# A two-level Strassen MLP kernel: a new written-out order of a pair, some sums moved to GpSimd, other buffers, and more of the second matmul begun in the drain

## The chip, the cores and the metric

The kernel runs on one core of a Trainium2 chip. TensorE (PE in the profile) does the matrix products, VectorE (DVE) and ScalarE (ACT) the work on their results, GpSimd (POOL) some element-wise sums and the stores, and SyncE (SP) issues the loads. The metric is the device time of one execution in microseconds (us), the median of the runs shown. Before the change it is 1467.58 us over three runs, from 1467.18 to 1467.59 us.

## The reference

Eight batches of 1024 rows go through a two-layer perceptron; everything is float32 outside and float16 inside the products.

```python
x: (8, 1024, 1024)   w1: (1024, 4096)   w2: (4096, 1024)
h = x @ w1
h = 0.5 * h * (1 + np.tanh(np.sqrt(2 / np.pi) * (h + 0.044715 * h ** 3)))
return (h @ w2).astype(np.float32)
```

## The kernel before

**Stages.** The eight batches are eight steps. Steps 0 and 1 use a one-level Strassen-Winograd scheme (seven block products in place of eight) and, beside it, prepare the sums of weights in DRAM. Steps 2 to 7 use two levels: each of the seven block products is again made of seven smaller ones. These six late steps are the same code: `matmul1_late` (L766) for x @ w1 with the GELU, then `matmul2` (L1113).

**The first matmul of a late step** goes over eight *pairs* j = 0..7 (a pair is 2 x 128 columns of each half of w1). The order of every instruction in a pair is written out by hand in the list `PAIR` (L30). One pass over the list is one pair; a token with a prime (') belongs to the pair before, so that the end of one pair lies among the beginning of the next. After pair 7 the list is gone through once more for its primed tokens alone: the *drain*. The instructions of each engine keep the order of the list. The tokens that matter here:

- `m` and two digits: one small product on TensorE, two matmuls of 256 columns (L704); `h`: four matmuls of 512 columns (L489). In pair 0 the products 1, 5 and 7 are not split; they are four matmuls of 512 columns per half (`whole`, L669).
- `z`, `e`, `s`, `u`: sums on VectorE that take a result out of a PSUM bank or put it into another; a following `m` that writes this bank again must wait for them. `c`, `a`, `p`, `q`: copies on ScalarE. `g`: the GELU on ScalarE into the tiles g11, g12, g21, g22.
- `v`: a sum on GpSimd; `d`: the difference of two chunks of g11 and g21, on GpSimd except in the first and the last pair (L758).
- `k`: a sum of weights, made on GpSimd for the next pair (L298). `b`: one quarter of the sum s7 of the second matmul, on GpSimd, in pairs 4 to 7 (L782, L1037).
- `x` and two digits: one inner sum of x on VectorE (`inner_sum`, L337). It is made once in a step: in pair 0 without a prime, in pair 1 with one. The inner sums of x2 are made ahead; in step 2 those of x3 too. The rest, 16 in steps 3 to 7, lie in pairs 0 and 1.

**The second matmul** has seven products in the order 4, 1, 2, 5, 6, 7, 3, and each has seven steps of 16 matmuls of 256 columns (`Inner.steps`, L1068). The sums it needs (`a`) and other VectorE jobs are placed behind given steps by the table `FILL_2` (L62). `n6` and `n3` there make x6 and x3 of the next batch; they stand behind the steps (3,6) and (3,7), the last two of all. Product 4 is begun early: four quarters of its first step are put into the drain in front of the tokens in `BEGIN` (L37). Its third step needs the sum s6, which VectorE makes as one instruction (`a46`) after the drain, behind the last pair's `d`.

**Buffers.** `up` has 26 buffers of 4 KB per partition (loads, operands, sums of weights), `gc` 5 of 4 KB (inner sums of x, s sums, staging of float32 weights in step 0), PSUM 8 banks. A load into `up` is issued as soon as a buffer is free.

Of the kernel before, what the change touches and what calls it, by code (L numbers as in the profile page):

```python
# [9 lines left out]
DT = mybir.dt.float16  # L10
# [50 lines left out]

FILL_2 = slots("""00:a46 a45  # L62
    ;41:a43;42:a17;43:a16;44:a15;45:a13;46:i2
# [4 lines left out]
    ;71:y11 y12;72:y21 y22;73:a37;74:a36 w11;75:a35 w12;76:a33 w21;77:w22  # L68
    ;31:z11 z12;32:z21 z22;36:n6;37:n3""".replace("\n    ", ""))


@with_exitstack
def kernel(
# [192 lines left out]
    class StoredHalf:  # L266
# [20 lines left out]
        def two(self, ks):  # L287
            two = self.room.pop(0) if self.room else up.tile([P, 2, KH * 2 * P], DT, name="u")
# [27 lines left out]
    class XOps(dict):  # L316
# [19 lines left out]

        def inner_sum(self, m, j):  # L337
            if m not in self.inner:
                self.inner[m] = gcp.tile([P, 4, 2, HT // 2], DT, name="gc")

            def operand(b):
                if isinstance(b, int):
                    return self.inner[m][:, SUMS.index(b)]
                k, t = int(b[0]) - 1, int(b[1]) - 1
                return self[m][:, 2 * k:2 * k + 2, t * HT // 2:(t + 1) * HT // 2]

            u, op, v = W_SUM[j]
            tt(operand(j), operand(u), operand(v), op, True)

# [314 lines left out]
    class Pair:  # L664
# [48 lines left out]
        def run(self, key):  # L713
# [34 lines left out]
            elif kind in "apq":  # L748
                act_copy(temp(kind, m), bank("a" if kind == "a" else "c", m))
            elif kind == "s":  # L750
                tt(temp("s", m), bank("a", m), temp("p", m), SUB, True)
            elif kind == "u":
                add(temp("p", m), bank("f", m), temp("s", m))
            elif kind == "v":
                t = temp("q", m)
                tc.keep_in_program_order(nc.gpsimd.tensor_tensor(out=t, in0=t, in1=temp("p", m), op=ADD))  # L756
            elif kind == "d":
                spare = 0 < self.j < NI // 2 - 1  # L758
                difference(self.g, self.j, nc.gpsimd if spare else nc.vector)
            else:  # L760
                b, h = key[1:3], int(key[3])
                src = {"11": bank, "12": bank, "21": temp, "22": temp}[b]
                src = src({"11": "b", "12": "d", "21": "q", "22": "p"}[b], h)
                gelu_into(self.g[b][:, 2 * self.j + h, :], src, -1.0 if b == "12" else 1.0)

    def matmul1_late(xs, sb, quads, g):  # L766
# [5 lines left out]
        for j in range(n + 1):  # L772
# [3 lines left out]
            for key in PAIR:  # L776
                late = key.count("'")
                key = key.rstrip("'")
                if key[0] == "x":
                    if late == j and int(key[1]) not in made:  # L780
                        xs.inner_sum(int(key[1]), int(key[2]))
                elif key == "b":  # L782
                    if 4 <= j < n:
                        early.quarter(j - 4)
                elif key[0] == "k":
# [220 lines left out]
    class Inner:  # L1006


        def __init__(self, m, t, rows=lambda a, t: None, part=lambda b, t: None, base=None):
            self.m, self.rows, self.part, self.base = m, rows, part, base  # L1010
            self.begun = None
            self.x, self.s, self.y = {b: inner_block(t, b) for b in BLOCKS}, {}, {}
# [17 lines left out]

        def make(self, j):
            u, op, v = S_SUM[j]
# [4 lines left out]
        def quarter(self, i):  # L1037

            if i == 0:
                self.s[7] = gcp.tile([P, NI // 2, HT // 2], GT, name="gc")  # L1040
            u, op, v = S_SUM[7]
            out, in0, in1 = (t[:, 2 * i:2 * i + 2, :] for t in (self.s[7], self.x[u], self.x[v]))
            tc.keep_in_program_order(nc.gpsimd.tensor_tensor(out=out, in0=in0, in1=in1, op=op))

        def multiply(self, j, bank, first):
            for n in range(4):
# [21 lines left out]
        def steps(self, into):  # L1068

            a, b, c = self.begun or psum(), psum(), psum()  # L1070
            for n, (j, bank, first, out, adds) in enumerate((
# [7 lines left out]
            ), 1):  # L1079
                if n > 1 or self.begun is None:  # L1080
                    self.multiply(j, bank, first)
                if out is not None:
                    t = quarter(into, out)
# [26 lines left out]
    def half():  # L1110
        return up.tile([P, 2, OH], F32, name="u")

    def matmul2(sb, g, early, nxt):  # L1113
# [21 lines left out]
        def run(key):  # L1135
            for job in FILL_2.get(key, ()):
# [3 lines left out]
                elif kind == "g":  # L1140
# [5 lines left out]
                    else:  # L1146
                        tt(g12, g12, g22, SUB, True)
                elif kind == "w":
                    add(4, 1, b)
# [12 lines left out]

        def claim():

            t = half()
            act_copy(t[:, 0, :1], warm)
            return t

        order = (4, 1, 2, 5, 6, 7, 3)
# [3 lines left out]
        for m, after in zip(order, order[1:] + (None,)):  # L1173
            into[m] = into[1] if m == 6 else [claim(), claim()]
            if after is not None:
# [62 lines left out]
```

## Time and profile before

| what | value |
|---|---|
| median of three runs | 1467.58 us |
| the profiled execution | 1467.73 us, of which the span of its instructions is 1466.0 us |
| busy share: PE / DVE / ACT / POOL | 99% / 84% / 46% / 39% |
| granted TensorE clock | 0.999 |
| one late step, from one first matmul to the next | 176.5 us |
| DMA | 472.70 MB, 322 GB/s |

Busy time is the time in which at least one instruction of an engine is in flight. Matmuls are pipelined, so that a PE that is busy all the time may still start its matmuls too late; the loss is read from the distance of their starts. In a run without a wait this distance is 0.216 us for 512 columns and 0.109 us for 256. In the timeline, a row gathers neighbouring instructions of one kind; the number in brackets is the idle time ahead of it and what ended it.

### The profile page before, as it was taken

The numbers are of one execution on the slowest core, as the hardware profiler recorded it, in microseconds if no ns is written. First come the engines' busy times: TensorE is split into PE (matmuls) and PEld (weight loads), VectorE is DVE, ScalarE is ACT, GpSimd is POOL, SyncE is SP. The second block draws the span as 40 slices with busy tenths as digits, with TensorE's granted clock in tenths as the row PEclk, the third lists the DMA queues.
The fourth block names the chain that finished last, engine by engine and source line by source line (L and its number), as shares of the span: only waits on it lengthen the run. The fifth ranks groups of instructions, "written<-read, shape, count | busy, mean of one in ns | idle before, by whom it ended". The sixth has DMA issues, their size and how long they took to land.

```text
span 1466.0 us, 28773 instructions
## 1 busy us (share of the span) xinstructions
PE 1455.0 (99%) x10635; PEld 1038.6 (71%) x10635; DVE 1227.9 (84%) x2064; ACT 675.5 (46%) x1406; POOL 568.8 (39%) x581
## 2 busy tenths in 40 slices
PE   9999999999999999999999999999999999999998
PEld 5444444444477888778877788777887778867787
DVE  5757768657778999989998899988999889898897
ACT  5666116631078511784128821388215872068510
POOL 2641232212358311691027811297104861148311
PEclk9999999999999999999999999999999999999999
DMA  9999999797999999989999999999999999996896
GB/s 338 388 373 373 245 370 338 256 278 241 354 368 215 327 328 368 376 227 367 326 371 366 210 392 315 364 346 234 395 346 358 307 278 354 355 392 239 322 290 207
DMA packets 205707, 472.70 MB, mean 322 GB/s; under 512 B 75648, under 2 KB 80768, under 8 KB 204672
## 3 DMA queue, kind: packets, MB, share of 16 engines
q1 hardware_dynamic: 177632, 373.35, 74.2%
q0 software_dynamic: 27936, 97.53, 22.4%
q8 instruction: 83, 1.36, 0.4%
q14 instruction: 56, 0.46, 0.1%
HBM read 370.15 MB, written 115.34 MB: 331 GB/s over the span
## 4 chain that ended last, share of the span: by engine, by line
PE 91%; DVE 5%; DMA 2%; issue 1%; ACT 0%; SPq 0%; DVEq 0%
PE ps L1059 33%; PE ps L489 22%; PE ps L704 22%; PE ps L1101 13%; DVE gc L136 2%; DVE u L136 1%; DVE tmp L136 1%; PE ps L422 1%; DMA g<-w_d 1%; DVE ps L136 1%; DMA u<-in_d 0%; ACT g L502 0%; PE ps L399 0%; DMA u<-in_x_dram 0%; PE ps L357 0%
## 5 line engine op out<-in xcount | busy, mean ns | idle before, releaser
L163 ACT COPY tmp<-ps 128x512 f32<-128x512 f32 (+1 forms) x536 | 272.5, 540 | 351.8 <-PE ps L489 177.5
L489 PE MATMUL ps<-u 128*128 128x512 f16 x1552 | 363.5, 379 | 0.8 <-DVE u L136 0.5
L704 PEld LDWEIGHTS <-u 128*128 128x128 f16 x2688 | 262.9, 98 | 65.4 <-issue 1.2
L1059 PE MATMUL ps<-u,gc 128*128 128x256 f16 x2688 | 300.4, 273 | 0.9 <-DVE gc L136 0.9
L1059 PEld LDWEIGHTS <-gc 128*128 128x128 f16 x2688 | 262.5, 98 | 32.9 <-DVE gc L136 2.6
L136 DVE TENSOR_TENSOR tmp<-tmp,ps 128x256 f32<-128x256 f32 (+1 forms) x372 | 197.0, 545 | 97.5 <-PE ps L1101 46.9
L489 PEld LDWEIGHTS <-u 128*128 128x128 f16 x1552 | 151.7, 98 | 147.9 <-DVE u L136 1.2
L827 POOL DMA_DIRECT2D out_dram<-u x70 | 63.9, 949 | 459.0 <-DVE u L136 245.1
L136 DVE TENSOR_TENSOR u<-u 128x512 f16<-128x512 f16 (+3 forms) x320 | 236.1, 782 | 4.3 <-DMA u<-w_d 1.4
L163 ACT COPY u<-ps 128x512 f32<-128x512 f32 (+1 forms) x134 | 78.0, 587 | 349.4 <-PE ps L1059 341.4
L704 PE MATMUL ps<-u 128*128 128x256 f16 x1520 | 232.4, 273 | 0.2
L1059 PE MATMUL ps<-u,g 128*128 128x256 f16 x2016 | 230.9, 273 | 0.0
L1059 PEld LDWEIGHTS <-g 128*128 128x128 f16 x2016 | 197.2, 98 | 22.8
L502 ACT ACTIVATE g<-tmp 128x512 f16<-128x512 f32 x282 | 178.7, 637 | 43.1 <-DVE tmp L136 43.0
L704 PE MATMUL ps<-gc,u 128*128 128x256 f16 x1168 | 189.2, 273 | 0.0
L136 DVE TENSOR_TENSOR ps<-tmp,ps 128x256 f32<-128x256 f32 x444 | 178.8, 423 | 11.7 <-PE ps L704 9.6
L136 DVE TENSOR_TENSOR u<-u,ps 128x512 f32<-128x512 f32 x216 | 147.7, 684 | 34.7 <-PE ps L1059 26.1
L1101 PE MATMUL ps<-u,g 128*128 128x512 f16 x768 | 166.4, 379 | 0.0
L756 POOL TENSOR_TENSOR tmp<-tmp 128x512 f32<-128x512 f32 x96 | 122.6, 1277 | 99.4 <-DVE tmp L136 46.8
L310 POOL TENSOR_TENSOR u<-u 128x512 f16<-128x512 f16 x120 | 136.1, 1155 | 27.3 <-PE ps L704 15.3
L502 ACT ACTIVATE g<-ps 128x512 f16<-128x512 f32 x230 | 138.3, 605 | 10.4 <-PE ps L704 3.9
L1101 PEld LDWEIGHTS <-g 128*128 128x128 f16 x768 | 75.2, 98 | 90.6
(53 smaller groups left out, 1146.5 us busy)
## 6 DMA issues: line engine op xcount, KB each, us to landing
u<-w_d SPq DMA_DIRECT2D x365, 512.0 KB, 10.2
u<-in_d SPq DMA_DIRECT2D x168, 512.0 KB, 8.3
out_dram<-u POOLq DMA_DIRECT2D x70, 512.0 KB, 11.3
gc<-in_w_dram SPq DMA_DIRECT2D x48, 512.0 KB, 7.8
g<-w_d SPq DMA_DIRECT2D x45, 512.0 KB, 12.6
w_d<-u POOLq DMA_DIRECT2D x40, 512.0 KB, 6.7
w_d<-u SPq DMA_DIRECT2D x32, 512.0 KB, 8.9
in_d<-u POOLq DMA_DIRECT2D x28, 512.0 KB, 7.2
```

What stands on the lines that cost most here:

```text
L136: i = nc.vector.tensor_tensor(out=out, in0=in0, in1=in1, op=op)
L163: tc.keep_in_program_order(nc.scalar.copy(out=out, in_=in_))
L310: nc.gpsimd.tensor_tensor(out=operand(j), in0=operand(u), in1=operand(v), op=op)
L422: tc.keep_in_program_order(nc.tensor.matmul(bank[:, cols], lhsT=w[:, k, :], rhs=self.xs.blocks[f"{a}{r}"][:, k, cols], start=r == 1 and k ...
L489: tc.keep_in_program_order(nc.tensor.matmul(bank, lhsT=w, rhs=x, start=first and k == 0, stop=k == n - 1, skip_group_check=not first,))
L502: gelu_last[0] = nc.scalar.activation(out=out, in_=src, func=GELU, scale=scale)
L704: tc.keep_in_program_order(nc.tensor.matmul(out, lhsT=w, rhs=x, start=first and k == 0, stop=k == 1, skip_group_check=not first,))
L756: tc.keep_in_program_order(nc.gpsimd.tensor_tensor(out=t, in0=t, in1=temp("p", m), op=ADD))
L827: return nc.gpsimd.dma_start(out=rows, in_=src, **kw)
L1059: tc.keep_in_program_order(nc.tensor.matmul(bank[:, i * OH // 2:(i + 1) * OH // 2], lhsT=t[:, c, i * P:(i + 1) * P], rhs=self.y[j][:, c, : ...
L1101: tc.keep_in_program_order(nc.tensor.matmul(pair(bank), lhsT=a[:, c, :], rhs=chunks(pieces[c // QC])[:, :, c % QC, :], start=(first and c ...
```

## The change

- `PAIR` is written in another order. Some tokens change sides (m35, m23, m22, z22 and the x sums x77, x17, x76 are now made in the pair itself; g220, h41, v0, s1 now come in the next one). Six inner sums of x, written `X`, go from VectorE to GpSimd: X35, X56 and X14 in pair 0, X37, X34 and X74 in pair 1.
- The sum s6 of the second matmul is made in quarters: r0, r1, r2 on GpSimd in pair 7 and the drain, the fourth on VectorE in place of `a46`.
- Five quarters are begun in the drain, four of product 4's first step and one of its second, and the copy of the first step's result is made there.
- The last pair's `d` moves from the drain behind `a45`. `n6` and `n3` move to behind (3,3) and (3,4).
- The sums of weights made with `k` get a pool of their own (`mp`, 2 buffers), x7's inner sums too (`xip`, 1); `up` falls from 26 to 24 and `gc` from 5 to 4. The sum of the sizes is the same.
- The pacing of the next batch's cast to DRAM watches other tiles.

```diff
-PAIR = """
-m51 m55 m35' x77' m11 q1' u1' m15 x17' z51 m36' m32' z22' g221' x54' m27' m23' m22' e30' z32'
-z11 m56 c1 z23' v1' z24' m12 x76' k7 g210' m16 x55 m33' g110' m52 c5 z12 m37' z52 m24' x15 e31'
-x75 g120' k5 m71 z33' m75 m13 z34' x37 m17 g111' m57 m53 z71 m21 c7 m25 m72 x56 x35 m76 m34' a0
-h60 z13 z53 x74' x14' m14 m54 p0 g211' z72 k6 g121' e20 d' m77 s0 m73 a1 x57 h40 p1 z73 u0 q0 v0
-e21 m31 x36 h61 z21 m74 x16 h41 z31 k3 g220 b x34 m26 s1
+X37' s1' g220' m11 g110' m15 u1' m36' m27' c1 e30' r1' X35 x55 m51 z11 z32' h41' m16 k7 z23'
+m32' m33' z24' z51 g221' x54' v0' k6 x15 m56 m55 z12 x36 m37' q1' g120' e31' x75 m71 X34' c5 m52
+z71 m24' m13 g111' z52 m12 m17 z33' m76 m75 z34' z13 m53 m57 v1' m21 m25 b a0 x17 h60 m34' z53
+c7 r0 p0 m14 x77 k5 g210' z72 k3 e20 m77 s0 g211' m54 z73 m73 X74' z21 m72 x57 a1 X56 h40 x16
+g121' m26 d' u0 z22 m31 p1 z31 x76 q0 e21 r2' h61 m74 m23 m22 m35 X14
-BEGIN = {"m33": (0,), "m24": (1,), "m34": (2, 3)}
+BEGIN = {"m32": (0,), "m33": (1,), "m24": (2, 3), "m34": (4,)}
...
-FILL_2 = slots("""00:a46 a45
+FILL_2 = slots("""00:a46 a45 d00
...
-    ;31:z11 z12;32:z21 z22;36:n6;37:n3""".replace("\n    ", ""))
+    ;31:z11 z12;32:z21 z22;33:n6;34:n3""".replace("\n    ", ""))
...
-    up = ctx.enter_context(tc.tile_pool(name="up", bufs=26))
+    up = ctx.enter_context(tc.tile_pool(name="up", bufs=24))
-    gcp = ctx.enter_context(tc.tile_pool(name="gcp", bufs=5))
+    gcp = ctx.enter_context(tc.tile_pool(name="gcp", bufs=4))
+    mp = ctx.enter_context(tc.tile_pool(name="mp", bufs=2))
+    xip = ctx.enter_context(tc.tile_pool(name="xip", bufs=1))
...
-        def inner_sum(self, m, j):
+        def inner_sum(self, m, j, engine=nc.vector):
             if m not in self.inner:
-                self.inner[m] = gcp.tile([P, 4, 2, HT // 2], DT, name="gc")
+                pool, name = (xip, "xi") if m == 7 else (gcp, "gc")
+                self.inner[m] = pool.tile([P, 4, 2, HT // 2], DT, name=name)
...
-                    nxt["xb"] = x_cast_paced(sb + 1, g["22"][:, 2 * j, :], 2 * j, nxt.get("xb"), True)
+                    done = g["22"][:, 2 * j - 1, :] if j else now.temps["a", 0]
+                    nxt["xb"] = x_cast_paced(sb + 1, done, 2 * j, nxt.get("xb"), True)
...
+        def make_quarter(self, j, i, engine=nc.gpsimd):
             if i == 0:
-                self.s[7] = gcp.tile([P, NI // 2, HT // 2], GT, name="gc")
+                self.s[j] = gcp.tile([P, NI // 2, HT // 2], GT, name="gc")
...
         def begin(self, n):
+            step, n = divmod(n, 4)
+            j = STEPS[step]
+            if step == n == 0:
+                self.into = [claim(), claim()]
             if n == 0:
-                self.begun = psum()
-            self.quarter_of(1, n, self.begun, True)
+                self.begun[j] = [psum(), 0]
+            bank, self.begun[j][1] = self.begun[j][0], n + 1
+            self.quarter_of(j, n, bank, True)
+            if (j, n) == (1, 3):
+                act_copy(quarter(self.into, "11"), pair(bank))
```

More of the change, by code (lines that the diff above doesn't have):

```diff
@@ L287, in two @@
         def two(self, ks):
-            two = self.room.pop(0) if self.room else up.tile([P, 2, KH * 2 * P], DT, name="u")
+            if ks == ("s1", "s5"):
+                two = mp.tile([P, 2, KH * 2 * P], DT, name="mu")
+            else:
+                two = self.room.pop(0) if self.room else up.tile([P, 2, KH * 2 * P], DT, name="u")
             if ks == ("s1", "s5"):
@@ L347, in inner_sum @@
             u, op, v = W_SUM[j]
-            tt(operand(j), operand(u), operand(v), op, True)
+            tc.keep_in_program_order(
+                engine.tensor_tensor(out=operand(j), in0=operand(u), in1=operand(v), op=op)
+            )
     def x_blocks():
@@ L757, in run @@
             elif kind == "d":
-                spare = 0 < self.j < NI // 2 - 1
-                difference(self.g, self.j, nc.gpsimd if spare else nc.vector)
+                if self.j < NI // 2 - 1:
+                    difference(self.g, self.j, nc.gpsimd if self.j else nc.vector)
             else:
@@ L778, in matmul1_late @@
                 key = key.rstrip("'")
-                if key[0] == "x":
+                if key[0] in "xX":
                     if late == j and int(key[1]) not in made:
-                        xs.inner_sum(int(key[1]), int(key[2]))
+                        xs.inner_sum(int(key[1]), int(key[2]), nc.vector if key[0] == "x" else nc.gpsimd)
                 elif key == "b":
                     if 4 <= j < n:
-                        early.quarter(j - 4)
+                        early.make_quarter(7, j - 4)
+                elif key[0] == "r":
+                    if j == n - 1 + late:
+                        early.make_quarter(6, int(key[1]))
                 elif key[0] == "k":
@@ L1010, in __init__ @@
             self.m, self.rows, self.part, self.base = m, rows, part, base
-            self.begun = None
+            self.begun, self.into = {}, None
             self.x, self.s, self.y = {b: inner_block(t, b) for b in BLOCKS}, {}, {}
@@ L1031, in make @@
         def make(self, j):
+            if j in self.s:
+                return self.make_quarter(j, 3, nc.vector)
             u, op, v = S_SUM[j]
@@ L1035, in make @@
             tt(self.s[j], in0, in1, op, True)
-        def quarter(self, i):
+        def make_quarter(self, j, i, engine=nc.gpsimd):
             if i == 0:
-                self.s[7] = gcp.tile([P, NI // 2, HT // 2], GT, name="gc")
-            u, op, v = S_SUM[7]
-            out, in0, in1 = (t[:, 2 * i:2 * i + 2, :] for t in (self.s[7], self.x[u], self.x[v]))
-            tc.keep_in_program_order(nc.gpsimd.tensor_tensor(out=out, in0=in0, in1=in1, op=op))
+                self.s[j] = gcp.tile([P, NI // 2, HT // 2], GT, name="gc")
+            u, op, v = S_SUM[j]
+            out, in0, in1 = (
+                (self.s[t] if isinstance(t, int) else self.x[t])[:, 2 * i:2 * i + 2, :] for t in (j, u, v)
+            )
+            tc.keep_in_program_order(engine.tensor_tensor(out=out, in0=in0, in1=in1, op=op))
         def multiply(self, j, bank, first):
-            for n in range(4):
+            for n in range(self.begun.get(j, (None, 0))[1], 4):
                 self.quarter_of(j, n, bank, first)
         def begin(self, n):
+            step, n = divmod(n, 4)
+            j = STEPS[step]
+            if step == n == 0:
+                self.into = [claim(), claim()]
             if n == 0:
-                self.begun = psum()
-            self.quarter_of(1, n, self.begun, True)
+                self.begun[j] = [psum(), 0]
[3 more added lines that the diff above has]
+                act_copy(quarter(self.into, "11"), pair(bank))
         def quarter_of(self, j, n, bank, first):
@@ L1068, in steps @@
         def steps(self, into):
-            a, b, c = self.begun or psum(), psum(), psum()
+            a, b = (self.begun[j][0] if j in self.begun else psum() for j in (1, 2))
+            c = psum()
             for n, (j, bank, first, out, adds) in enumerate((
@@ L1079, in steps @@
             ), 1):
-                if n > 1 or self.begun is None:
-                    self.multiply(j, bank, first)
-                if out is not None:
+                self.multiply(j, bank, first)
+                if out is not None and (self.into is None or n > 1):
                     t = quarter(into, out)
@@ L1111, in half, with claim @@
         return up.tile([P, 2, OH], F32, name="u")
+    def claim():
+        t = half()
+        act_copy(t[:, 0, :1], warm)
+        return t
     def matmul2(sb, g, early, nxt):
@@ L1147, in run @@
                         tt(g12, g12, g22, SUB, True)
+                elif kind == "d":
+                    difference(g, NI // 2 - 1)
                 elif kind == "w":
@@ L1161, in run @@
                     nxt.make_inner(m)
[L1163 to L1167, printed above, removed]
         order = (4, 1, 2, 5, 6, 7, 3)
@@ L1173, in matmul2 @@
         for m, after in zip(order, order[1:] + (None,)):
-            into[m] = into[1] if m == 6 else [claim(), claim()]
+            into[m] = into[1] if m == 6 else products[m].into or [claim(), claim()]
             if after is not None:
```

## The prediction

> **What bounds the kernel now.** I read the page first: TensorE is busy throughout, at full granted clock.
>
> ```profile
> span 1466.0 us, 28773 instructions
> PE 1455.0 (99%) x10635; PEld 1038.6 (71%) x10635; DVE 1227.9 (84%) x2064; ACT 675.5 (46%) x1406; POOL 568.8 (39%) x581
> ...
> PEclk9999999999999999999999999999999999999999
> ```
>
> The change neither adds nor takes away a matmul, so only late starts can be won or lost. I therefore went through the timeline of PE and took, between neighbouring matmuls, the distance of their starts less 0.109 us (256 columns) or 0.216 us (512). From 37.6 us on, nothing above 0.025 us is lost outside the six late steps, and inside them only at two places. The first is the beginning of steps 3 to 7, here of step 6, which starts at 1108.78 us:
>
> ```profile
> 1121.03 0.38 PE L704 MATMUL ps<-gc,g 128*128 128x256 f16 x2
> 1121.88 0.60 PE L704 MATMUL ps<-u,g 128*128 128x256 f16 x4 [0.47 <-DVE ps L136]
> 1122.32 0.38 PE L704 MATMUL ps<-gc,g 128*128 128x256 f16 x2
> 1122.67 0.60 PE L704 MATMUL ps<-u,g 128*128 128x256 f16 x4
> ```
>
> Two matmuls from 1121.03 take 0.22, so the next could start at 1121.25; it starts at 1121.88, released by VectorE: 0.64 lost. Two from 1122.32 last to 1122.54; the next starts at 1122.67: 0.14. With 0.13 ahead (1119.94) and 0.08 behind (1126.25) it is 0.99 us, and the same in each of steps 3 to 7. Step 2, whose x3 sums are ready, loses nothing here. The second place is the drain of all six:
>
> ```profile
> 1200.91 0.38 PE L704 MATMUL ps<-gc,u 128*128 128x256 f16 x2
> 1201.13 1.91 PE L1059 MATMUL ps<-u,g 128*128 128x256 f16 x16
> 1203.19 1.05 PE L1059 MATMUL ps<-u,gc 128*128 128x256 f16 x8 [0.15 <-DVE gc L136]
> ```
>
> Sixteen matmuls from 1201.13 take 1.75, to 1202.88; the third step starts at 1203.19: 0.32 lost. 0.19 (m27 at 1197.78) and 0.08 (m34 at 1200.91) make 0.59 us. What released them, on VectorE:
>
> ```profile
> 1201.31 0.69 DVE L508 TENSOR_TENSOR g<-g,g 128x1024 f16<-128x1024 f16 x1 [0.45 <-DMA u<-in_d]
> 1201.92 1.22 DVE L136 TENSOR_TENSOR gc<-g,gc 128x2048 f16<-128x2048 f16 x1
> ```
>
> The whole s6 (1.22) stands behind the last pair's `d`. So 5 x 0.99 + 6 x 0.59 = 8.5 us is all that can be had. Then the engines at a step's start, by windows of pairs 0, 1 and 3:
>
> ```profile
> core 0: us, PE busy (x) PEld busy (x) DVE busy (x) ACT busy (x) POOL busy (x), PEclk, DMA share, GB/s
> 1108.80:1119.90 11.10, 11.10 (x64) 6.05 (x62) 11.10 (x25) 4.54 (x9) 4.26 (x7) 1.00 1.05 374
> 1119.90:1131.00 11.10, 10.63 (x79) 7.59 (x78) 10.79 (x26) 8.79 (x19) 2.65 (x5) 1.00 1.02 374
> 1142.00:1153.10 11.10, 11.10 (x89) 8.41 (x86) 9.27 (x23) 9.20 (x21) 10.23 (x11) 1.00 1.02 368
> ```
>
> VectorE is full in pairs 0 and 1 while GpSimd has 6.8 and 8.4 us free; from pair 3 on it is GpSimd that is full. Last, a GpSimd sum and a VectorE sum of two SBUF tensors side by side:
>
> ```profile
> 1116.14 1.26 POOL L756 TENSOR_TENSOR tmp<-tmp 128x512 f32<-128x512 f32 x1 [5.37 <-DVE gc L136]
> 1116.34 1.35 DVE L136 TENSOR_TENSOR gc<-u,gc 128x512 f16<-128x512 f16 x1
> ...
> 1110.04 0.73 POOL L827 DMA_DIRECT2D out_dram<-u  x1 [0.84 <-DVE u L136]
> ```
>
> The VectorE sum, 0.42 alone, ends 0.29 after the GpSimd one: it waited. Of 44 such sums in the late steps the 11 that met a GpSimd sum took 1.18 on average, the other 33 took 0.42. Sums that read PSUM show no difference (0.423 either way).
>
> **The change, part by part.**
>
> *Drain.* s6's first three quarters go to GpSimd (1.155 each, the row of the s7 quarters at L1043), the fourth (0.42, as any 128x512 float16 sum) stays on VectorE, now ahead of `d` (0.69). After m34, PE has 0.22 of m34 and three quarters of the second step (12 x 0.109 = 1.31) before it asks for s6; the fourth quarter, begun at the latest when m34's z34 is done, needs 0.42 of these 1.53. GpSimd's last quarter (r2) is asked for another 0.44 later, by the second quarter of the third step; in the trace GpSimd's v1 of the drain ends 1.9 us before m34, and 1.155 behind it is in time even if v1 comes 2 us later. So 0.32 goes to zero. m27 comes in the new order some 2 us after its z22, which is made in the pair itself: 0.19 goes too. m34 still follows m37, e31, z33, z34 with the same 1.53 us of matmuls between m37 and m34 (m24 and three quarters, before and after), so its 0.08 stays. Win 0.51 per step, six times: 3.1 us. Bounds: 1.9 (only 0.32 won) to 3.5 us (all 0.59). r0 waits for a `gc` buffer, which m14 or m54 of pair 7 frees; behind it on GpSimd stand only pair 6's `d` and r1, whose first readers are some us away. The two claims (0.19 each) and the copy (0.59) that ScalarE now makes in the drain stand behind g220 and g110; the GELUs behind them (but g221, needed by s6's last quarter some 2 us later) feed product 1 and later ones.
>
> *Start of a step.* VectorE loses six sums of x (spacing 0.334: 2.0 us); n6 and n3 (1.135 each) move from the last two steps of product 3 to its third and fourth, where per step of 1.75 us stand 0.60 + 1.135. That takes 4.3 us off a queue that is 0.99 us late. The new danger is a chain: VectorE's x36 needs X35 from GpSimd, and X35 stands behind the second store of the last product, issued at 1110.04 + 0.73 = 1.99 us after the step's start. X35 then ends at 1.99 + 1.11 = 3.10, X56 follows at once until 4.20, and x36, which starts while X56 runs, ends 0.28 behind it at 4.48. Behind it come x75, x17, x77, e20 (0.334 each), s0 (0.60) and z21 (0.42), which ends at about 6.76. PE reaches m26, which writes z21's bank again, after seven products of 0.863 and two of 0.218: 6.48. So about 0.33 with the signal's 0.05 is lost there, and later ones (m33 by z32, m13 by z12) come within 0.1 us of their time or earlier. Win 0.66 in five steps: 3.3 us. Bounds: nothing lost (5.0 us) if X35 goes ahead of that store, which nothing but readiness orders; 0.0 if the later sums meet GpSimd as well (below).
>
> Here the skill can be set beside the row. A moved sum takes 1.155 us on GpSimd against 0.42 on VectorE, 2.8 times. The Trainium skill, GPSIMD Engine Reference, section Engine selection, advises against GpSimd for sums of two inputs and puts them at about twice VectorE's time. By that factor, an estimate, X35 and X56 would take 0.84 each, x36 would end 0.5 us earlier, nothing would be lost at m26, and the sum below would be 1.7 us less. The row decides.
>
> *A steady pair.* Same instructions; the pacing copies and the two casts to DRAM behind each (0.51 per issue on GpSimd) stay behind pairs 0 to 3, where GpSimd has room, and their readers come in pairs 4 to 7. Laid out with these rows, the nearest result before a waiting matmul lies 0.39 us ahead in the new order (z32 before m32), against 0.27 in the old one (z24 before m24), which shows no loss. Zero; the cover is that margin.
>
> *Buffers.* Four `gc` buffers hold the four s sums of a product. `a17` must now wait for s6 of product 4, one step (1.75) longer; behind it on VectorE wait the sums of product 1, first read 12 us later. With 24 `up` buffers the weights of the second matmul are asked for at most two steps (3.5 us) later; the shortest time from landing to use in that stage is 6.1 us. Zero. In step 0 one staging load less is ahead: the load issued at 10.01 waits for the cast that ends at 10.54, and the one issued at 17.39 for the cast that ends at 24.06. PE loses 1.1 us around 36 to 37.6 behind sums that GpSimd's casts hold up (1.5 in place of 0.69 each). Later casts may help by one such wait (-0.8) or a load may slip by one landing (+1.4); I take 0.
>
> *Sum.* The profiled execution, 1467.73, less 3.1 and 3.3 is 1461.3; it stands 0.15 above the median, so 1461.2.
>
> **Rivals.**
>
> *The port takes back the gain at the start* (1466.0 us). Each of the six moved sums meets a VectorE sum: 6 x 0.76 = 4.6 us of waiting against 4.3 taken off, so 1.3 us is lost instead of 0.99: 1467.6 - 3.1 + 5 x 0.3 = 1466.0. For it: 11 of 44 met before, and pair 1 now has three more GpSimd sums. Against: fewer VectorE sums of that kind are left to meet (10). The Trainium skill, SBUF — State Buffer, section Who interferes with whom, says that whoever starts first holds the shared port for the whole instruction, and that the other is blocked fully. By that rule each meeting costs the rest of the GpSimd sum; the trace agrees (1.18 against 0.42).
>
> *The smaller `up` pool stops VectorE in steps 0 and 1* (about 1472 us). There VectorE writes 16 inner sums of weights into `up` buffers, in order (205 to 307 us), while loads take every free buffer. A sum that finds none waits for PE's next product, 4 x 2 x 0.216 = 1.73 us; PE feels what exceeds VectorE's free time, 0.3 us in pair 1 of step 1 (11.81 busy of 12.10) and 1.5 to 3.4 in its neighbours. Six waits that PE feels are 10.4 us: 1461.2 + 10.4 = 1471.6. It decides from 9.3 us on (6.4 + 2.9). For it: loads in that stage already wait for buffers. Against: the trace has no VectorE wait for a buffer there.
>
> *X35 goes ahead of the stores*: 1459.6, by the bound above.
>
> **How the numbers follow.** The forecast has 0.55, X35 ahead 0.13, the port 0.16, the pool 0.16. The range goes from 1458.8 (everything at both places won, and 0.5 in step 0) to 1468.2: it leaves out the pool's case and a little of the port's. A measurement of this kernel can tell about 0.2%, 2.9 us. Faster by more (below 1464.6): the forecast and X35 ahead; 0.68. Slower by more (above 1470.5): the pool, 0.15. The port's case, 0.16, and the rest are within: 0.17.
>
> **What would show it.** Right: at a drain, the third step follows the second without a gap; at a step's start, one wait of some 0.3 us at m26, and steps 175.1 to 175.5 us apart instead of 176.5. Wrong: gaps of PE between 37 and 404 us, VectorE waiting for a DMA or for PE's buffers there, VectorE's x sums of 1.2 us in pairs 0 and 1 with PE waiting behind them, or a wait in every pair.

## The result, and the profile after

The changed kernel is slower: 1485.34 us, the median of four executions (1482.05 to 1492.48), against 1467.38 us for the kernel before; the ratio is 1.013, with a 95% interval of 1.0093 to 1.0167. The forecast was 1461.2, and its range ended at 1468.2. The profiled execution took 1482.05 us, so it stands 14.3 us above the one profiled before. The page after the change:

```profile
span 1480.3 us, 28812 instructions
PE 1455.5 (98%) x10635; PEld 1038.9 (70%) x10635; DVE 1223.9 (83%) x2031; ACT 690.4 (47%) x1406; POOL 622.0 (42%) x632
...
PEclk9999999999999999999999999999999999999999
```

TensorE still has the same 10635 matmuls, so the 14.3 us are starts that came late, or matmuls that ran at a lower clock. I took the distances of neighbouring starts again. What was forecast to be won is there. The drain of step 6, in the timeline of PE (start, busy time, engine, line, operation, number):

```profile
1216.62 0.38 PE L712 MATMUL ps<-gc,u 128*128 128x256 f16 x2
1216.84 1.47 PE L1082 MATMUL ps<-u,g 128*128 128x256 f16 x12
1218.15 1.04 PE L1082 MATMUL ps<-u,gc 128*128 128x256 f16 x8
```

Twelve matmuls from 1216.84 take 1.31, to 1218.15, and the third step starts there: no gap. Each of the six drains lost 0.59 us before and loses 0.08 now. At the start of step 6 one wait is left, at m26:

```profile
1126.15 0.59 PE L497 MATMUL ps<-u,g 128*128 128x512 f16 x2
1127.00 0.60 PE L712 MATMUL ps<-u,g 128*128 128x256 f16 x4 [0.26 <-DVE ps L138]
```

Two matmuls of 512 columns take 0.43, so the next was due at 1126.58: 0.41 lost at this place, in steps 3, 4, 6 and 7; 1.00 in step 5.

What the forecast did not have comes 10 us later in steps 3 to 6. Step 3 starts at 582.56 us; the timelines of PE, VectorE and GpSimd in its pair 1:

```profile
595.64 0.71 PE L712 MATMUL ps<-u,g 128*128 128x256 f16 x5
599.21 0.38 PE L712 MATMUL ps<-u,mu 128*128 128x256 f16 x2 [2.86 <-DVE ps L138]
```

```profile
594.09 0.88 DVE L138 TENSOR_TENSOR ps<-tmp,ps 128x256 f32<-128x256 f32 x2
594.88 3.94 DVE L355 TENSOR_TENSOR gc<-u,gc 128x512 f16<-128x512 f16 x1
598.75 0.41 DVE L138 TENSOR_TENSOR ps<-tmp,ps 128x256 f32<-128x256 f32 x1
```

```profile
592.19 0.51 POOL L472 DMA_DIRECT2D xb<-in_x_dram  x1
592.71 1.18 POOL L355 TENSOR_TENSOR gc<-u 128x512 f16<-128x512 f16 x1
593.83 1.28 POOL L764 TENSOR_TENSOR tmp<-tmp 128x512 f32<-128x512 f32 x1
595.06 1.16 POOL L355 TENSOR_TENSOR gc<-u,gc 128x512 f16<-128x512 f16 x1
596.17 1.26 POOL L764 TENSOR_TENSOR tmp<-tmp 128x512 f32<-128x512 f32 x1
597.39 1.14 POOL L355 TENSOR_TENSOR xi<-u,xi 128x512 f16<-128x512 f16 x1
598.48 0.38 POOL L477 COPY pace<-g 128x2 f16<-128x2 f16 x1
```

The VectorE instruction of 3.94 us is x54, one of the sums that take 0.42. GpSimd makes X37, v0, X34, v1 and X74 without a gap between them, and x54 ends 0.29 us behind the last. The sums queued behind it (598.75 and on) are what PE waits for: 3.02 us. The same stands at 777.66, 956.71 and 1136.76. In step 7, which has no cast of a next batch, x54 took 0.43 and nothing was lost.

The other new place is step 0. The timelines of PE, of VectorE and of the stores in SyncE's queue there, and VectorE's waits from 140 to 200 us (instruction, what it waited for, us in total, times, longest):

```profile
193.74 1.24 PE L1124 MATMUL ps<-u,g 128*128 128x512 f16 x5
197.76 5.51 PE L1124 MATMUL ps<-u,g 128*128 128x512 f16 x17 [2.79 <-DVE tmp L138]
```

```profile
194.68 2.43 DVE L138 TENSOR_TENSOR u<-u 128x1024 f16<-128x1024 f16 x3 [8.63 <-DMA w_d<-u]
197.03 2.47 DVE L138 TENSOR_TENSOR tmp<-tmp,ps 128x512 f32<-128x512 f32 x4
```

```profile
191.36 3.57 SPq L162 DMA_DIRECT2D w_d<-u  x4
```

```profile
DVE u L138 <- DMA w_d<-u: 20.9, 2, 12.3
```

VectorE wants an `up` buffer for a sum of the second matmul's weights, and the buffer comes free when its old content has been stored; the store was issued at 191.36 and landed at 194.59. It is one of those that SyncE issues between the loads, so it comes later when the loads ahead of it do. PE loses 2.95 us. Before the change VectorE had no wait of this kind.

The account of the profiled executions, in us:

| place | before | after | difference |
|---|---|---|---|
| six drains | 3.5 | 0.5 | -3.1 |
| m26 and its neighbours, steps 3 to 7 | 5.0 | 2.7 | -2.3 |
| around 37 us | 1.1 | 0 | -1.1 |
| PE behind x54, steps 3 to 6 | 0 | 12.1 | +12.1 |
| step 0, near 198 us | 0 | 2.9 | +2.9 |
| step 2, near 417 us | 0 | 0.9 | +0.9 |
| matmuls at half rate (199, 957 and 1138 us) | 0 | 4.7 | +4.7 |
| sum | | | +14.1 |

The last row: for some 3 us behind one wait in step 0, one in step 5 and one in step 6 the starts of 512 columns lie 0.427 apart in place of 0.216, and those of 256 columns 0.213 in place of 0.109; the granted clock is 0.50 there. The four executions took 1482.05, 1484.81, 1485.87 and 1492.48 us at mean granted clocks of 0.996, 0.996, 0.995 and 0.993. A mean clock that is lower by 0.003 over 1490 us is, by estimate, 4.5 us more lost at half rate, of the 10.4 us between the first and the last. The loss in step 0 varies too: three of the runs below have the same steps 0 and 1 and lose 5.38 to 8.94 us there in place of 2.95. Only the fastest of the four has a profile.

### The profile page after: what moved, and what is told of

It reads as the page before. It is cut to its first block, busy times and chain, and to the rows that moved or that the text cites. A ratio compares the mean times of both kernels' runs of the same rounds, so it can differ in the third digit from the quotient of the medians.

```text
span 1480.3 us, 28812 instructions
## 1 busy us (share of the span) xinstructions
PE 1455.5 (98%) x10635; PEld 1038.9 (70%) x10635; DVE 1223.9 (83%) x2031; ACT 690.4 (47%) x1406; POOL 622.0 (42%) x632
## 3 DMA queue, kind: packets, MB, share of 16 engines
q8 instruction: 83, 1.36, 0.4%
## 4 chain that ended last, share of the span: by engine, by line
PE 68%; DVE 3%; issue 1%; DVEq 0%
PE ps L1082 35%; PE ps L712 22%; PE ps L497 11%; DVE tmp L138 1%; DVE gc L355 1%; DVE ps L138 1%; DVE xi L355 0%; DVE u L138 0%; DVEq L138 0%
## 5 line engine op out<-in xcount | busy, mean ns | idle before, releaser
L165 ACT COPY tmp<-ps 128x512 f32<-128x512 f32 (+1 forms) x536 | 280.6, 536 | 294.9 <-PE ps L1124 139.2
L497 PEld LDWEIGHTS <-u 128*128 128x128 f16 x1552 | 152.1, 98 | 146.8 <-issue 0.5
L138 DVE TENSOR_TENSOR u<-u 128x1024 f16<-128x1024 f16 (+3 forms) x292 | 221.2, 800 | 36.2 <-DMA w_d<-u 20.9
L712 PEld LDWEIGHTS <-u 128*128 128x128 f16 x2026 | 197.7, 98 | 48.1 <-issue 0.8
L712 PE MATMUL ps<-u 128*128 128x256 f16 x1342 | 204.9, 273 | 0.3 <-DVE tmp L138 0.2
L510 ACT ACTIVATE g<-tmp 128x512 f16<-128x512 f32 x282 | 173.4, 634 | 47.0 <-DVE tmp L138 46.7
L138 DVE TENSOR_TENSOR tmp<-ps,tmp 128x512 f32<-128x512 f32 x126 | 87.0, 690 | 55.9 <-PE ps L497 45.9
L138 DVE TENSOR_TENSOR gc<-g,gc 128x2048 f16<-128x2048 f16 x78 | 95.0, 1218 | 0.6
(68 smaller groups left out, 1470.4 us busy)
```

Of the source, the lines that this page charges most:

```text
L138: i = nc.vector.tensor_tensor(out=out, in0=in0, in1=in1, op=op)
L165: tc.keep_in_program_order(nc.scalar.copy(out=out, in_=in_))
L497: tc.keep_in_program_order(nc.tensor.matmul(bank, lhsT=w, rhs=x, start=first and k == 0, stop=k == n - 1, skip_group_check=not first,))
L510: gelu_last[0] = nc.scalar.activation(out=out, in_=src, func=GELU, scale=scale)
L712: tc.keep_in_program_order(nc.tensor.matmul(out, lhsT=w, rhs=x, start=first and k == 0, stop=k == 1, skip_group_check=not first,))
```

## The experiments

Theory A for the 12.1 us, built on the shared port of the prediction's rival: a VectorE sum of two SBUF tensors waits through a whole series of GpSimd sums that follow each other without a gap. The runs can show this waiting, not the port itself. Its rival B: x54 waits for something of its own (data, a buffer), or GpSimd simply has too much to do. For step 0 the theory was the pool of 24, its rival the pool of 4.

### A break in the series

```diff
-... X34' c5 ... v1' ...
+... X34' G c5 ... v1' ...      # G in pair 1: one small DMA issue on GpSimd
```

> The changed kernel with one more DMA issue on GpSimd (4 bytes per partition to a scratch in DRAM, some 0.5 us) between its sums X34 and v1 in pair 1 of steps 2 to 6; VectorE's work is the same. Theory A (GpSimd keeps the SBUF port it shares with VectorE through a series of sums that follow each other without a gap): VectorE's x54 gets its turn in the gap and ends 0.29 us behind X34, so it takes some 1.6 us in place of 3.94; the loss at 16.6 us after the start of steps 3 to 6 falls from 3.02 to about 0.7 us each, and the profiled span falls from 1480.3 by 9 to 12 us, though GpSimd has 0.5 us more to do. Rival B (x54 waits for its data or its buffer, or GpSimd simply has too much): 3.94 and 3.02 stay, or grow by 0.5.

Measured: the timelines of VectorE and GpSimd, step 3.

```profile
600.69 2.05 DVE L356 TENSOR_TENSOR gc<-u,gc 128x512 f16<-128x512 f16 x1
600.87 1.15 POOL L356 TENSOR_TENSOR gc<-u,gc 128x512 f16<-128x512 f16 x1
601.97 0.58 POOL L790 DMA_DIRECT2D mark_d<-warm  x1
602.57 1.29 POOL L765 TENSOR_TENSOR tmp<-tmp 128x512 f32<-128x512 f32 x1
```

x54 took 2.05 and no longer waited for v1, and the loss fell from 3.02 to 1.14 in each of the four steps. A holds against B; the size is off by 0.4, since x54 ended 0.7 behind X34 and not 0.29, but 0.2 behind the added issue: it waited on through this one. The execution as a whole took 1511.54 us: step 0 lost 8.94, and PE waited up to 5 us for loads of weights. In step 3 the added transfer of 4 bytes per partition landed at 614.46 and a load of weights, issued at 586.63, at 614.67, 26.3 us after the step's start; the load that landed 18.3 us after the start in the changed kernel had been issued at 580.11. Whether the added transfer held the load up is not shown. So only the local reading counts, not the time.

### A series that is one sum shorter

```diff
-... m73 X74' z21 ...
+... m73 x74' z21 ...
```

> The changed kernel with the sum X74 of pair 1 back on VectorE, at its place in the list; so the series of GpSimd sums that x54 meets is one shorter and ends with v1 (at 597.43 us in the profile of the changed kernel, 594.88 being x54's start). Theory A: x54 ends 0.29 behind v1 and takes about 2.8 us in place of 3.94; the loss in steps 3 to 6 falls from 3.02 to about 1.9 us. If the small copy that paces the cast holds the port as well (0.38), 3.2 and 2.3. Rival B (its data, its buffer): 3.94 and 3.02 stay.

Measured (VectorE and GpSimd, step 3):

```profile
597.29 2.85 DVE L355 TENSOR_TENSOR gc<-u,gc 128x512 f16<-128x512 f16 x1
597.47 1.16 POOL L355 TENSOR_TENSOR gc<-u,gc 128x512 f16<-128x512 f16 x1
598.58 1.26 POOL L764 TENSOR_TENSOR tmp<-tmp 128x512 f32<-128x512 f32 x1
599.79 0.38 POOL L477 COPY pace<-g 128x2 f16<-128x2 f16 x1
```

x54 ends 0.30 behind v1 (599.84), not behind the small copy, and the loss is 1.93 us in all four steps. One sum less, 1.1 us less: this is theory A in its numbers. The gain was taken back elsewhere (1482.12 us): 5.81 lost in step 0, and 0.75 to 1.16 at some 33 us after the start of steps 3 to 6, where GpSimd's first made sum of weights waited for a load.

### 26 up buffers again, and x54 on GpSimd

```diff
-    up = ... bufs=24      mp = ... bufs=2
+    up = ... bufs=26      # made sums of weights from up
```

> The changed kernel with 26 up buffers, the made sums of weights being taken from them as before the change; gc stays at 4, x7's inner sums keep their own buffer, the order stays. Theory: the pool of 24 alone lets VectorE wait in step 0, so the loss of 2.95 us at 197.76 us and the eight matmuls at half rate behind it (1.69) go: 4.6 us less than the changed kernel, a profiled span near 1475.7, and nothing changes at the starts of the steps (3.02 in steps 3 to 6). Rival (the gc pool of 4, or the order, is behind that wait): the wait stays, span near 1480.

The second kernel has in addition `x54'` written `X54'`:

> The kernel of e3 (26 up buffers) with the sum x54 of pair 1 on GpSimd as well, behind v0: VectorE then has no sum of two SBUF tensors beside that series, and GpSimd's series is one sum (1.16 us) longer. Theory A with the pool's: both new losses go, 1480.3 less 4.6 (step 0), less 4 x 3.02 (steps 3 to 6), less about 3.5 (matmuls at half rate behind two of the waits) leaves a span near 1460, a time near 1462, ratio 0.996. Rival (GpSimd is then late by 1.16 with v1, X34 or X74, and PE waits for their readers): up to 1.2 us lost in each of five steps, time near 1467, ratio 1.000. Rival B (the time is the moved sums' own, wherever they run): no better than 1480.

Both expectations failed in the whole and held at their places. The times are 1528.87 us (ratio 1.0424, 1.0407 to 1.0441) and 1541.37 us (1.0496, 1.0466 to 1.0526). In the first the loss near 198 us is gone and the 3.02 us stay; in the second x54 no longer holds anything up. But every late step has new waits of 1.45 to 3.75 us in its later pairs. GpSimd and PE in such a pair of the first:

```profile
659.21 1.16 POOL L311 TENSOR_TENSOR u<-u 128x512 f16<-128x512 f16 x1 [3.96 <-DVE ps L137]
660.32 1.27 POOL L760 TENSOR_TENSOR tmp<-tmp 128x512 f32<-128x512 f32 x1
```

```profile
665.61 0.38 PE L708 MATMUL ps<-u 128*128 128x256 f16 x2 [2.85 <-ACT g L506]
```

The made sum (L311) waits, 3.96 us here, and v, the GELU behind v and PE follow. Between the first kernel and the changed one only the pool of the made sums differs (26 `up` buffers for both uses, in place of 24 and 2), so the pool of its own is what lets the new order, with k7 early in the pass, run without a wait. In the second kernel PE also lost 3.9 us in step 0, at a load of weights near 213 us.

### The pools alone, in the kernel before

```diff
-    up = ... bufs=26
+    up = ... bufs=24      mp = ... bufs=2
```

> The kernel before with one part of the change alone: up falls from 26 to 24 buffers and the made sums of weights get a pool of their own (2); order, gc and everything else as before. Theory (the pool of 24 stops VectorE in step 0): TensorE loses 2.9 to 8.9 us near 198 us, as the changed kernel and its variants do, with some 1.2 to 1.7 us of matmuls at half rate behind it; time 1471 to 1477, ratio 1.003 to 1.007. Rival (the gc pool of 4 is the cause): no loss there, ratio 1.000.

```diff
-    gcp = ... bufs=5
+    gcp = ... bufs=4      xip = ... bufs=1
```

> The kernel before with another part alone: gc falls from 5 to 4 buffers and x7's inner sums get a buffer of their own; up stays at 26. It is the other half of the comparison with the kernel of 24 up buffers. Theory (24 up buffers are the cause in step 0): ratio 1.000, within 0.1%. Rival (gc): a loss of 2.9 us or more near 198 us or, as the variant with 26 up and 4 gc buffers and x54 on GpSimd showed it in its profile, 3.9 us near 213 us at a load of weights; ratio 1.003 or more.

Measured: 1468.62 us, ratio 1.0009 (1.0000 to 1.0018), and 1467.75 us, ratio 1.0010 (0.9999 to 1.0022). Neither profile has a loss near 198 us; with 4 `gc` buffers PE loses 0.45 at 211 and 0.90 at 222 us. Three of the ten executions with 4 `gc` buffers took 1470.57 to 1475.20 us, the slowest at a clock of 0.997; the profiled one took 1467.56, so what those lost is not known. My theory that 24 `up` buffers alone stop TensorE fell. What each does is seen in the queue of loads (SP), at the first load of the second matmul's weights, `u<-in_w_dram`. In order: the kernel before, the changed kernel, 24 `up`, 4 `gc`.

```profile
99.80 9.13 SPq L160 DMA_DIRECT2D u<-in_w_dram  x8
```

```profile
106.82 4.86 SPq L162 DMA_DIRECT2D u<-in_w_dram  x6
```

```profile
101.99 8.91 SPq L161 DMA_DIRECT2D u<-in_w_dram  x8
```

```profile
109.93 1.53 SPq L161 DMA_DIRECT2D u<-in_w_dram  x3
```

One staging buffer less puts the whole queue 7 to 10 us back by 100 us; two `up` buffers less let VectorE wait for stored tiles (9.10 us, until 192.04, in the run with 24, which PE does not yet feel). Only the profiles with both show PE waiting there. In every profile with 24 `up` buffers VectorE's wait ends 3.2 to 3.3 us behind the first of the four stores that SyncE issues in a row (191.36 above). With five `gc` buffers this store is issued at 186.98 to 189.19 us, and PE loses nothing (three profiles); with four, at 191.36 to 197.30, and PE starts again 3.1 us behind VectorE, 2.95 to 8.94 us late (five profiles).

### x54 at the head of the pass, and two tiles of step 0 from the idle pool

```diff
+x54' X37' s1' g220' ...          # and x54' taken out behind g221'
...
-[unit(2, HALF) for _ in range(NI // QC)]
+[unit(2, HALF) if n < 2 else mp.tile([P, 2, HALF], DT, name="mu") for n in range(NI // QC)]
```

> The changed kernel with two repairs at places far apart. In step 0 and 1 two of the four tiles of the fifth sum of the second matmul's weights come from the pool of the made sums, which lies idle there: by the pool theory the loss near 198 us goes (4.6 us with the half rate in the profile of the changed kernel), by its rival it stays. In the late steps x54 of pair 1 stays on VectorE and moves to the head of the pass, ahead of the GpSimd sums X37, v0, X34, v1, X74: by theory A it takes 0.42 us (at most 1.4, where it meets X37), and the 3.02 us at 16.6 us after the start of steps 3 to 6 go. What the loads allow then: the first made sum of weights waits for a load that lands 25.8 us after the step's start in the changed kernel, and a pass that is 3 us earlier waits longer for it; in the variant without X74 on GpSimd this cost 1.2 to 1.5 us at 33 us after the start. So 1466 to 1470, ratio 0.999 to 1.002. Rival B (x54 waits for what it reads): 1480 or more.

Both repairs failed: 1495.10 us, ratio 1.0193 (1.0176 to 1.0211). Step 0 lost 5.22 us all the same: VectorE still waited for a stored tile, 15.01 us, until 196.96. And x54 met the series at its head, with 4.0 us lost on PE in each of steps 3 to 6 (VectorE and GpSimd):

```profile
594.27 1.06 POOL L472 DMA_DIRECT2D xb<-in_x_dram  x2
594.53 4.59 DVE L355 TENSOR_TENSOR gc<-u,gc 128x512 f16<-128x512 f16 x1
595.34 1.18 POOL L355 TENSOR_TENSOR gc<-u 128x512 f16<-128x512 f16 x1
596.45 1.27 POOL L764 TENSOR_TENSOR tmp<-tmp 128x512 f32<-128x512 f32 x1
597.67 1.15 POOL L355 TENSOR_TENSOR gc<-u,gc 128x512 f16<-128x512 f16 x1
599.04 0.68 DVE L138 TENSOR_TENSOR tmp<-ps,tmp 128x512 f32<-128x512 f32 x1
```

It ends 0.30 behind X34 (598.82), where the series now breaks: v1 waits 3.94 us, by the profile for a copy of ScalarE. The waiting of A is seen a third time, but the expectation that x54 would be first was wrong: it began 0.8 us before X37, while GpSimd issued the cast's DMAs, and still waited. Why is open (last section).

### x54 behind the series, and the fifth gc buffer

```diff
-    gcp = ... bufs=4      xip = ... bufs=1
+    gcp = ... bufs=5
...
-... g221' x54' v0' ... m34' z53
+... g221' v0' ... m34' z53 x54'
```

> The changed kernel with two repairs. gc has 5 buffers again and x7's inner sums come from it, up stays at 24 and the made sums keep their pool: the runs so far say that neither 24 up buffers nor 4 gc buffers alone stop TensorE for long in step 0, so the loss of 2.95 us near 198 us (and its half rate, 1.69) should go with the fifth gc buffer. If it stays, something else of the change is behind it. And x54 of pair 1 stays on VectorE, but behind z53, some 3 us later, where the series v0, X34, v1, X74 is nearly over: by theory A it ends at most 0.3 us behind X74 (598.53 us, or 16.0 after the step's start, in the profile of the changed kernel), ahead of its reader m54 (some 16.6 to 16.9), and the sums that feed the matmuls are no longer behind it: 3.02 us less in each of steps 3 to 6, a loss of 0 to 0.5 in its place. Behind that the weights' loads: the kernel with X74 on VectorE lost 1.2 to 1.5 us per step at 33 us, behind a sum of weights on GpSimd that waited for its load; the same or up to 3 us here. So a time of 1463 to 1472. Rival B (x54 waits for something of its own): it waits here too.

Measured: 1476.37 us, ratio 1.0057 (1.0041 to 1.0072). Both of the large losses are gone: nothing near 198 us, so the fifth `gc` buffer settles step 0 with 24 `up` buffers, and nothing behind x54. Rival B fell. What is left is the loads' part, larger than expected: 1.3 to 3.2 us at 29 to 31 us after the start of steps 3 to 6, 1.16 behind it in three of them, and 2.6 us of half rate behind the 3.2. GpSimd and PE in step 3 (start 578.98):

```profile
606.93 1.14 POOL L314 TENSOR_TENSOR mu<-u 128x512 f16<-128x512 f16 x1 [10.67 <-PE ps L710]
```

```profile
610.22 1.01 PE L710 MATMUL ps<-gc,u 128*128 128x256 f16 x4 [3.08 <-DVE ps L137]
```

The made sum is put down to PE, but its operand's load landed at 606.80, 0.13 ahead of it. The v sums stand behind it on GpSimd. In the changed kernel the same wait (8.63 us, until 608.44) lay under the 3 us that PE had already lost. Step 7, without casts, loses nothing there.

### The casts one pair later

```diff
-                if j < 4:
-                    done = g["22"][:, 2 * j - 1, :] if j else now.temps["a", 0]
-                    ... x_cast_paced(sb + 1, done, 2 * j, ...)
+                if 0 < j < 5:
+                    done = g["22"][:, 2 * j - 1, :]
+                    ... x_cast_paced(sb + 1, done, (4, 6, 0, 2)[j - 1], ...)
```

> The changed kernel with the casts of the next batch to DRAM (a pacing copy and two DMA issues on GpSimd) behind pairs 1 to 4 in place of 0 to 3, the rows in the order in which the transposes of pairs 4 to 7 need them. Theory A says that this copy and these issues (1.4 us) in front of X37 are what makes the sums X37, v0, X34, v1, X74 follow without a gap: without them, as in step 7, which has no cast, each v waits for its own data, a gap opens and x54 takes 0.4 to 1.6 us in place of 3.94; so the 3.02 us in steps 3 to 6 fall to 0 to 0.7. Rival B: 3.94 stays. Step 0 is untouched (2.9 to 8.9 us lost near 198 us). Casts that come later may be late for the transposes, or crowd GpSimd in pair 4; at the start of a step the weights' loads have fewer transfers beside them. Span 1468 to 1475.

Measured: 1472.20 us, span 1470.4. The sums of the changed kernel, all in their places (VectorE and GpSimd, step 3):

```profile
594.63 0.41 DVE L355 TENSOR_TENSOR xi<-u,xi 128x512 f16<-128x512 f16 x1
594.70 1.36 POOL L355 TENSOR_TENSOR gc<-u 128x512 f16<-128x512 f16 x1
...
597.25 1.15 POOL L355 TENSOR_TENSOR gc<-u,gc 128x512 f16<-128x512 f16 x1
597.47 0.88 DVE L138 TENSOR_TENSOR ps<-tmp,ps 128x256 f32<-128x256 f32 x2
598.26 0.42 DVE L355 TENSOR_TENSOR gc<-u,gc 128x512 f16<-128x512 f16 x1
598.53 1.28 POOL L764 TENSOR_TENSOR tmp<-tmp 128x512 f32<-128x512 f32 x1
```

X34 ends at 598.40, v1 starts at 598.53, and x54, which begins 0.14 before the end of X34, takes 0.42. No step loses anything behind x54, and step 2's 0.9 us are gone too. So it was the cast of the next batch, a copy and two DMA issues in front of X37, that brought about the long wait. x54 begins 12.32 us after the step's start in both kernels, X37 10.15 us after it in the changed one and 8.76 here: x54 falls on the end of X34 and not into v0. That the gap of 0.13 us behind X34 let it through, as the expectation has it, is not shown: the VectorE sum at 594.63 also began just before the end of a GpSimd sum (594.74), and took 0.41 though X37 followed at 594.70 without a gap and itself took 1.36 in place of 1.18. Step 0 lost 5.38, as the untouched part had to; 1.7 us were lost twice at loads in the second matmul and 1.06 once in a pair.

### Both causes repaired

The casts of the last run and the fifth `gc` buffer; all else as in the changed kernel.

> The changed kernel with both causes repaired and nothing else touched: 5 gc buffers, x7's inner sums among them (step 0), and the casts one pair later (steps 3 to 6); the order, the sums on GpSimd, 24 up buffers and the own pool of the made sums stay. If these two are the whole difference from the prediction, the losses of the changed kernel (2.95 and 1.69 in step 0, 4 x 3.02, some 3.5 of half rate, 0.9 in step 2) are gone and the span of 1480.3 becomes 1459.6, a time near 1461, ratio 0.996. What the kernel with the later casts alone lost besides, 1.7 us twice at loads in the second matmul and 1.06 once in pair 2, may stay: then 1465, ratio 0.9985. If the loads become the limit of a faster start, as in the kernel with x54 behind z53, 1468 or more.

Measured: 1465.07 us, the median of twelve, ratio 0.9991 (0.9982 to 1.0001): 20.3 us less than the changed kernel, not told apart from the kernel before, and the middle one of the three expectations. In the profiled execution (span 1463.0) there is no half rate, no wait near 198 us, none behind x54; the drains lose 0.08 and m26 0.41, in step 5 too. Left over are 1.55 and 0.97 at loads in the second matmul and 1.16 in a pair, 3.7 us together; the profiled execution, 1464.76 us, stands 3.6 above the forecast. The steps without these are 175.44 and 175.45 us apart.

### d, n6 and n3 alone

```diff
-FILL_2 = slots("""00:a46 a45
+FILL_2 = slots("""00:a46 a45 d00
...
-    ;31:z11 z12;32:z21 z22;36:n6;37:n3"""
+    ;31:z11 z12;32:z21 z22;33:n6;34:n3"""
```

> The kernel before with two short parts of the change alone, on VectorE only: the last pair's d behind the second s sum (behind a45), and n6 and n3 behind (3,3) and (3,4). No sum goes to GpSimd, pools and order stay. Expected: s6 starts 1.06 us earlier in each drain, 0.32 less in each of six (m27's 0.19 and m34's 0.08 stay); at the start of steps 3 to 7 VectorE has 2.27 us less queued where it is 0.99 us late, so that all or most of the 0.99 goes. 6 x 0.32 + 5 x 0.99 = 6.9 us at the most, time 1460.5 to 1462, ratio 0.9955 to 0.997. Rival (the moved x sums are what frees VectorE, and n6 and n3 were hidden): 1.9 us from the drain alone, time 1465.5, ratio 0.9987.

Measured: 1463.39 us, ratio 0.9973 (0.9963 to 0.9984): less than the kernel before, by an interval below 1, with none of the sums moved to GpSimd and no new pool. The 0.32 in front of the third step is gone from all six drains. At the starts 0.99 became 0.63, less than expected; what holds the rest is a meeting again (VectorE and GpSimd, step 3):

```profile
588.70 1.29 POOL L756 TENSOR_TENSOR tmp<-tmp 128x512 f32<-128x512 f32 x1
588.83 1.45 DVE L136 TENSOR_TENSOR gc<-u,gc 128x512 f16<-128x512 f16 x1
```

That is x54 beside v1. The last run moves it behind v1:

```diff
-... g221' x54' m27' ... m12 x76' k7
+... g221' m27' ... m12 x76' x54' k7
```

> The kernel before with d and n6, n3 moved as in the run of those two parts (1463.4 us), and x54 of pair 1 moved behind x76, one GpSimd sum later: in that run's profile x54 took 1.45 us beside v1 (588.70 to 589.99) and was the one long sum in front of the 0.41, 0.14 and 0.08 us that are still lost at the start of steps 3 to 7. From 589.99 to 598.45 GpSimd has nothing. Expected: x54 takes 0.42, VectorE is 1.0 us earlier where it is 0.41 late, and 5 x 0.6 = 3.0 us go: time near 1460.4, ratio 0.9955. Rival (other VectorE work behind x54 then waits, or x54 is late for m54): 0 to 1 us gained, ratio 0.997.

Measured: 1462.19 us, ratio 0.9965 (0.9952 to 0.9977). x54 takes 0.42, and the starts of steps 3 to 7 lose 0.25 to 0.31 in place of 0.63; 0.2 came back in step 2. It gains 1.2 us on the run before, not 3.0, and the intervals of the two overlap; both lie below 1.

## Why the prediction was wrong

**Drain: right.** 3.1 us were forecast and 3.06 found, by the steps named: the 0.32 at the third step, the 0.19 at m27, and m34's 0.08 stayed. The run of `d`, n6 and n3 got the 0.32 by the move of `d` alone, without s6 in quarters on GpSimd.

**The wait at m26: right in place and cause, the size 0.08 off.** 0.33 forecast, 0.41 found. In step 5 the last stores were issued 0.6 us later, X35 with them, and the loss was 1.00. So 2.3 us were won there and not 3.3.

**"Later ones come within 0.1 us of their time or earlier": wrong, and the largest term.** The working let x36 wait for the rest of the one GpSimd sum that it meets (0.28 behind X56; 1.36 us in the trace, so this meeting was right), and the price of a meeting, 0.76, came from the kernel before, where each VectorE sum met a single one. In the new order five GpSimd sums follow one another in pair 1; a VectorE sum that begins among them had to be priced by the series and not by one sum: 3.94 - 0.42 = 3.52 us on VectorE, 3.02 on PE, four times. The bound of 0.0 for this term, and the rival of the port (six meetings of 0.76, 1466.0), had the right mechanism with the same too small price. The Trainium skill, SBUF — State Buffer, section Who interferes with whom, gives the lock for the whole instruction; that much the trace bears out, but by that rule x54 would have ended 0.29 us behind v0, 0.5 us after its start, and it sat through four sums.

**"In step 0 one staging load less is ahead ... I take 0": wrong.** I followed the staging to 37 us only, and there it did win 1.1 us, a little more than the bound of 0.8. But the buffers are used to 105 us, in order, and the delay adds up to 7 us by the first load behind them; PE then lost 2.95 us near 198 us, and 1.7 by half rate behind it. **"With 24 `up` buffers ... Zero"** looked at the second matmul of the late steps alone. The rival of the pool named the right kind of wait (VectorE without a buffer), but its place, the inner sums at 205 to 307 us, and its releaser, a matmul, were wrong: it was the sums of the second matmul's weights, released by stores. And it needed the smaller `gc` beside it, which no rival had. The trace of the kernel before could have shown this: follow the loads of step 0 in order, with one buffer less, to their end.

**"A steady pair ... zero": right in the changed kernel, but its cover was misnamed.** No steady pair lost anything. Yet pair 2 holds a wait of GpSimd for a load, which the 3 us lost ahead of it covered; the runs without that loss paid up to 3.2 us there. I had named a margin of 0.39 between results and matmuls, none of loads.

**The half rate** was in no term: it came behind three of the five waits of 3 us, and I had forecast none of these.

The steps 175.1 to 175.5 us apart, forecast as the sign of a right prediction, are found nowhere in the changed kernel (178.4 to 180.6). With the casts moved two of four distances are 175.4; the old order with `d`, n6, n3 and x54 moved has 175.45 to 175.50 in all four, so this sign did not tell the new order from a shorter change.

## What to carry to other kernels

When a sum moves from VectorE to GpSimd, look at what stands next to it on GpSimd: a sum of VectorE with two SBUF inputs that begins inside an unbroken series can wait for the end of the whole series, and so do the short sums behind it. What stands ahead of the series (copies, DMA issues) decides where in it the sum falls. And a pool that loses a buffer has to be followed through the whole in-order queue that it feeds, not only at its first waits; a short change that undoes one wait (`d` behind one sum, 1.9 us) can be worth more than a new order.

## What the runs showed of the hardware

- A VectorE sum of two SBUF tensors (128x512 float16, 0.42 us alone) took 2.85, 3.94 and 4.59 us beside unbroken series of GpSimd sums, and ended 0.29 to 0.30 us behind the last sum in each. In these traces it depends on where the sum begins. In steps 2 to 7 of all profiles 59 such sums began 0.10 to 0.15 us before the end of a GpSimd sum and took 0.40 to 0.43, 17 of them with the next GpSimd sum right behind. Another 17 began 0.22 us or more before that end, with the next sum right behind: 16 waited on for it, and one (1320.61 us in the run with x54 at the head) passed, while the next GpSimd sum took 1.44. Sums of 256 columns that read PSUM ran at 0.41 to 0.43 beside the same series.
- Two such sums began while GpSimd issued the first DMA of a cast, with a series right behind the issues, and waited through it too: the 4.59 above, and 2.23 at 414.22 us of the changed kernel. Others that began as the second issue started took 0.41. With an issue between two sums of the series, x54 ended 0.2 us behind the issue in all four steps. Whether the issue itself holds such a sum up, or the GpSimd sum behind it does so early, stays open.
- Matmuls at half rate for some 3 us came behind two of the four waits of 3.02 us, behind the four of 4.0 us (x54 at the head) and behind none of the four of 1.93; in the changed kernel they cost 1.5 and 1.6 us, and 1.7 behind the 2.95 in step 0. The Trainium skill, TensorE: Matmul & The Clock Gate, Part 1: The HAM clock gate, describes an activity window of 3.4 us that runs freely, and half the clock after an idle window. Waits of 3.02 us are shorter than that window and were still followed by half rate in steps 5 and 6, though not in 3 and 4; what tells these apart is not shown.
